# A two-layer transformer block in float32 by split products: in the second layer the high weights take both token parts in one 512-column product

## The chip, the cores and the metric

The kernel runs on one core of one Trainium2 chip. The metric is the time of one execution on the device in microseconds (us); smaller is better. Three runs of the kernel before took 2539.17, 2540.15 and 2541.22 us, a median of 2540.15 us.

## The reference, cut to what matters

Two streams of 256 tokens with 1024 features each, latent and context, go through two layers. Each layer is a half feed-forward block, a mixer and another half feed-forward block. After the mixer of the second layer only the latent stream is used.

```python
DEPTH, D_MODEL, SEQ, CTX_LEN, FF = 2, 1024, 256, 256, 2816

def _swiglu(h, w_in, w_out):
    a, b = jnp.split(h @ w_in, 2, axis=-1)
    return (jax.nn.silu(a) * b) @ w_out

def _half_ffn(h, shift, scale, gate, w1, w2, g, b):
    y = _swiglu(h * (1 + scale) + shift, w1, w2)
    return _layer_norm(DN_ALPHA * h + 0.5 * gate * y, g, b)

def _gated_merge(branches, gates, w_branch, w_out):
    g = jax.nn.sigmoid(gates.reshape(B, T, N_BRANCH, D_MODEL))
    proj = jnp.einsum('btkw,kwd->btkd', br, w_branch)
    return jnp.einsum('btkd,btkd->btd', g, proj) @ w_out

for l in range(DEPTH):
    last = l == DEPTH - 1
    xl = _half_ffn(xl, ...); xc = _half_ffn(xc, ...)
    yl, yc = _mixer(hl, hc, rows, cols, not last, ...)   # LRU, windowed GQA, MLA, retention, merged
    xl = _half_ffn(_layer_norm(DN_ALPHA * xl + ml[5] * yl, ...), ...)
    if not last:
        xc = ...                                         # the same for the context
```

## The kernel before, in words

Activations are kept transposed: a tile has 128 features on the partitions and tokens in the free dimension, latent in columns 0 to 255 and context in 256 to 511. A float32 product is made of three float32r products. Every operand is split into a high and a low part (`split` for activations, `load_w` for weights: ScalarE casts the high part, VectorE subtracts it to get the low part), and `mm3` issues high weights times high tokens (L189), high weights times low tokens (L190) and low weights times high tokens (L191). Such a group of three is called a triple here. The low times low product is dropped.

`gemm_cols` walks a weight matrix in pairs of 128-column blocks. Weights come in units of 512 KB (four feature tiles by 256 columns) over SyncE's DMA queue into three raw buffers and go through the split into four buffers of high and low parts. A pair accumulates in two of four PSUM tiles called `acc`, and then a function of the caller takes each block out of PSUM (the eviction): a ScalarE activation for `silu`, `tanh` and plain copies, a VectorE operation where two operands meet (L568 in the feed-forward block, L1170 in a merge).

In the first layer nearly all products have 512 columns. In the second layer the query-side products of the mixer (`bq`, `cq`, `ay`, `dq`, `dg`, the gates `gt`, the branch projections and `w_out`) and the whole second feed-forward block `ffn11` are for the latent stream alone, so their three products have 256 columns each. There are 1128 such triples: 528 in `ffn11`, 408 against the mixer's input (56 in `gqa_in`, 32 in `lru_out`, 64 in `ret`, 64 in each of the four merges), 128 against the branches (32 in each merge) and 64 in `finish`.

Names that come back below: `gqa_in` makes queries and keys of the windowed attention, `lru` is a VectorE-heavy recurrence that is interleaved with the gate products of `merge1`, `mla` is the second attention, `ret` the retention, `finish` the product with `w_out` and its LayerNorm. A scheduler at build time sets the order of each engine's instructions from the program and its own estimates; on the chip each engine then works its list strictly in that order.

## Time and profile before

| | |
|---|---|
| median of three runs | 2540.15 us (2539.17 to 2541.22) |
| span of the profiled execution | 2538.8 us |
| TensorE busy, modelled | 2453.9 us, 97% |
| TensorE weight loads busy | 2046.2 us, 81% |
| VectorE busy | 1620.2 us, 64% |
| ScalarE busy | 1048.8 us, 41% |
| GpSimd busy | 390.6 us, 15% |
| granted TensorE clock, mean | 0.990 of 2.4 GHz |

No time of the profiled execution is listed other than its span. It lies 1.35 us below the median of the runs, so changes that are worked out against the span are added to the median as they are. PE is TensorE, PEld its weight loads, DVE VectorE, ACT ScalarE, POOL GpSimd and SP SyncE. A line number such as L189 is a line of the kernel before. The busy time of TensorE counts the length of each matmul, and neighbours overlap, so it says that matmuls were in flight and not how fast they follow one another.

### The profile page before, as it was taken

The numbers are of one execution on the slowest core, as the hardware profiler recorded it, in microseconds if no ns is written. First come the engines' busy times: TensorE is split into PE (matmuls) and PEld (weight loads), VectorE is DVE, ScalarE is ACT, GpSimd is POOL, SyncE is SP. The second block draws the span as 40 slices with busy tenths as digits, with TensorE's granted clock in tenths as the row PEclk, the third lists the DMA queues.
The fourth block names the chain that finished last, engine by engine and source line by source line (L and its number), as shares of the span: only waits on it lengthen the run. The fifth ranks groups of instructions, "written<-read, shape, count | busy, mean of one in ns | idle before, by whom it ended". The sixth has DMA issues, their size and how long they took to land.

```text
span 2538.8 us, 35128 instructions
## 1 busy us (share of the span) xinstructions
PE 2453.9 (97%) x13320; PEld 2046.2 (81%) x13320; DVE 1620.2 (64%) x3288; ACT 1048.8 (41%) x1694; POOL 390.6 (15%) x411
## 2 busy tenths in 40 slices
PE   8999999999999999999999999999999999999997
PEld 5888788666776778898877898877886777998997
DVE  4756438768757676467665386664387986766554
ACT  4322226556435322352223252223265754455443
POOL 2000024003111112350000230000240121223002
PEclk9999999999999999999999999999999999999999
DMA  7554334122423334426554346664352342465653
GB/s 262 167 157 149 125 106 149 36 75 84 126 85 91 93 107 138 136 84 190 155 166 141 96 139 210 196 193 156 100 149 68 92 126 75 119 186 162 190 179 113
DMA packets 304027, 340.75 MB, mean 134 GB/s; under 512 B 13505, under 2 KB 262625, under 8 KB 303857
## 3 DMA queue, kind: packets, MB, share of 16 engines
q1 hardware_dynamic: 299600, 323.88, 42.0%
q0 software_dynamic: 4256, 14.63, 1.6%
q8 instruction: 104, 1.70, 0.3%
q14 instruction: 67, 0.54, 0.1%
HBM read 334.26 MB, written 4.20 MB: 133 GB/s over the span
## 4 chain that ended last, share of the span: by engine, by line
PE 69%; DVE 12%; DMA 12%; issue 3%; ACT 3%; POOL 1%; SPq 0%; POOLq 0%; DVEq 0%; ACTq 0%
DMA ffn10.mraw<-in_w_modT 4%; PE ffn01.acc L189 3%; PE ffn01.acc L191 3%; PE ffn01.acc L190 3%; DMA ffn00.mraw<-in_w_modT 3%; PE ffn00.acc L189 3%; PE ffn00.acc L191 3%; PE ffn00.acc L190 3%; PE ffn11.acc L189 3%; PE ffn11.acc L190 3%; PE ffn11.acc L191 3%; DMA ffn01.mraw<-in_w_modT 2%; PE ffn10.acc L189 2%; PE ffn10.acc L190 2%; PE ffn10.acc L191 2%
## 5 line engine op out<-in xcount | busy, mean ns | idle before, releaser
L189 PE MATMUL ffn10.acc<-xh,ffn10.hi 128*128 128x512 f32 (+1 forms) x384 | 141.9, 376 | 7.2 <-DVE ffn10.sa L568 5.0
L189 PE MATMUL ffn01.acc<-xh,ffn01.hi 128*128 128x512 f32 (+1 forms) x384 | 140.5, 374 | 7.9 <-DVE ffn01.sa L568 7.9
L176 ACT CAST ffn10.hi<-ffn10.raw 128x1024 fp32r<-128x1024 f32 (+1 forms) x71 | 72.7, 1024 | 173.4 <-DMA ffn10.raw<-in_ffn_w_in 95.8
L190 PE MATMUL ffn10.acc<-xl,ffn10.hi 128*128 128x512 f32 (+1 forms) x384 | 142.2, 373 | 0.0
L191 PE MATMUL ffn10.acc<-xh,ffn10.lo 128*128 128x512 f32 (+1 forms) x384 | 142.1, 373 | 0.0
L190 PE MATMUL ffn01.acc<-xl,ffn01.hi 128*128 128x512 f32 (+1 forms) x384 | 141.3, 372 | 0.0
L191 PE MATMUL ffn01.acc<-xh,ffn01.lo 128*128 128x512 f32 (+1 forms) x384 | 141.1, 372 | 0.0
L189 PE MATMUL ffn00.acc<-xh,ffn00.hi 128*128 128x512 f32 x336 | 133.4, 398 | 4.7 <-ACT ffn00.hi L176 2.8
L177 DVE TENSOR_TENSOR ffn10.lo<-ffn10.raw,ffn10.hi 128x1024 fp32r<-128x1024 f32 (+1 forms) x71 | 87.4, 1231 | 74.6 <-ACT ffn10.hi L176 74.5
L176 ACT CAST ffn01.hi<-ffn01.raw 128x1024 fp32r<-128x1024 f32 (+1 forms) x71 | 72.6, 1023 | 148.5 <-DMA ffn01.raw<-in_ffn_w_in 70.9
L177 DVE TENSOR_TENSOR ffn01.lo<-ffn01.raw,ffn01.hi 128x1024 fp32r<-128x1024 f32 (+1 forms) x71 | 87.9, 1239 | 72.0 <-ACT ffn01.hi L176 70.3
L177 DVE TENSOR_TENSOR ffn00.lo<-ffn00.raw,ffn00.hi 128x1024 fp32r<-128x1024 f32 (+1 forms) x71 | 86.4, 1218 | 73.0 <-ACT ffn00.hi L176 72.8
L190 PE MATMUL ffn00.acc<-xl,ffn00.hi 128*128 128x512 f32 x336 | 132.3, 394 | 0.0
L191 PE MATMUL ffn00.acc<-xh,ffn00.lo 128*128 128x512 f32 x336 | 132.0, 394 | 0.0
L177 DVE TENSOR_TENSOR ffn11.lo<-ffn11.raw,ffn11.hi 128x1024 fp32r<-128x1024 f32 x68 | 82.3, 1211 | 75.7 <-ACT ffn11.hi L176 75.7
L176 ACT CAST ffn00.hi<-ffn00.raw 128x1024 fp32r<-128x1024 f32 (+1 forms) x71 | 72.4, 1023 | 136.5 <-PE ffn00.acc L190 88.5
L401 DVE SCALAR_TENSOR_TENSOR ffn10.ht<-ffn10.mraw,ffn10.sb 128x512 bf16<-128x512 f32 x128 | 83.6, 687 | 66.3 <-DMA ffn10.mraw<-in_w_modT 62.6
L401 DVE SCALAR_TENSOR_TENSOR ffn01.ht<-ffn01.mraw,ffn01.sb 128x512 bf16<-128x512 f32 x128 | 82.3, 688 | 67.8 <-DMA ffn01.mraw<-in_w_modT 67.7
L401 DVE SCALAR_TENSOR_TENSOR ffn00.ht<-ffn00.mraw,ffn00.sb 128x512 bf16<-128x512 f32 x96 | 62.1, 687 | 70.3 <-DMA ffn00.mraw<-in_w_modT 70.3
L189 PE MATMUL ffn11.acc<-xh,ffn11.hi 128*128 128x256 f32 x352 | 99.7, 287 | 4.8 <-ACT xh L246 4.8
L190 PE MATMUL ffn11.acc<-xl,ffn11.hi 128*128 128x256 f32 x352 | 100.3, 286 | 0.0
L191 PE MATMUL ffn11.acc<-xh,ffn11.lo 128*128 128x256 f32 x352 | 100.1, 286 | 0.0
(682 smaller groups left out, 7826.1 us busy)
## 6 DMA issues: line engine op xcount, KB each, us to landing
ffn10.mraw<-in_w_modT SPq DMA_DIRECT2D x48, 512.0 KB, 4.2
ffn00.raw<-in_ffn_w_in SPq DMA_DIRECT2D x44, 512.0 KB, 3.7
ffn01.raw<-in_ffn_w_in SPq DMA_DIRECT2D x44, 512.0 KB, 4.5
ffn10.raw<-in_ffn_w_in SPq DMA_DIRECT2D x44, 512.0 KB, 4.6
...
```

The costliest lines, as they stand in the source:

```text
L176: nc.scalar.copy(out=hi[:, :n], in_=raw[:, :n])
L177: nc.vector.tensor_tensor(out=lo[:, :n], in0=raw[:, :n], in1=hi[:, :n].bitcast(F32), op=ALU.subtract)
L189: mm(out, wh, xh, start=start, stop=False)
L190: mm(out, wh, xl, start=False, stop=False)
L191: mm(out, wl, xh, start=False, stop=stop)
L401: nc.vector.scalar_tensor_tensor(out=junk, in0=raw[:, e], scalar=1.0, in1=sb[:, i], op0=ALU.mult, op1=ALU.mult, accum_out=dst)
```

## The change

The high and the low part of a set of tokens no longer lie in two tiles. One tile holds `[stream, part, 256]`, so that for one stream high and low are 512 neighbouring columns. Where a product is for the latent stream alone, the high weights meet these 512 columns in one matmul (PSUM columns 0 to 255 get high times high, 256 to 511 high times low), and the low weights meet the high tokens in a second matmul of 256 columns that adds to the first half. Each such block is then summed over its two halves by a new VectorE reduce, `done`, into a buffer in SBUF, and the caller's eviction reads that buffer. Where a product is for both streams the three matmuls stay, but their 512 columns of tokens are now two runs of 256 that lie 512 columns apart. The pools keep their sizes, save that eight tiles of `g` replace sixteen of `q` in `finish` of the second layer.

```diff
+class Split:
+    def __init__(self, t=None, h=None, l=None):
+        self.t = t
+        if t is None:
+            self.H, self.L = (x.rearrange("p (s t) -> p s t", t=L) for x in (h, l))
+        else:
+            self.H, self.L = t[:, :, 0], t[:, :, 1]
+    def hl(self, s):
+        return None if self.t is None else self.t[:, s]
+def by_stream(x):
+    return x.rearrange("p (s t) -> p s t", t=L)
...
-        def block(a, i, m, units, t):
+        def block(a, i, m, units, s=None):
             sl = slice(i * 128, i * 128 + m)
+            mm = self.nc.tensor.matmul
+            a3 = by_stream(a)
             for kk, h, lw in units:
-                self.mm3(a[:m, t], h[:, sl], lw[:, sl], xh[kk][:, t], xl[kk][:, t], kk == 0, kk == kt - 1)
+                st, sp = kk == 0, kk == kt - 1
+                if s is None:
+                    self.mm3(a3[:m], h[:, sl], lw[:, sl], x[kk].H, x[kk].L, st, sp)
+                elif both:
+                    self.mm3(a3[:m, s], h[:, sl], lw[:, sl], x[kk].H[:, s], x[kk].L[:, s], st, sp)
+                else:
+                    mm(a3[:m], h[:, sl], x[kk].hl(s), start=st, stop=False)
+                    mm(a3[:m, 0], lw[:, sl], x[kk].H[:, s], start=False, stop=sp)
+        def done(a):
+            if both:
+                return a
+            r = self.ht(1)
+            self.nc.vector.tensor_reduce(out=r, in_=a.rearrange("p (x t) -> p t x", x=2), axis=AX.X, op=ALU.add)
+            return r
...
-                evac(b0 + i, a, (0, 1) if both else (0,))
+                evac(b0 + i, done(a), (0, 1) if both else (0,))
...
-        self.xh = [self.p_x.tile([128, T], F32R, name=f"xh{d}") for d in range(KD)]
-        self.xl = [self.p_x.tile([128, T], F32R, name=f"xl{d}") for d in range(KD)]
+        self.x = [Split(self.p_x.tile([128, 2, 2, L], F32R, name=f"x{d}")) for d in range(KD)]
...
-                            t = ph.tile([128, 2, T], F32R, tag=f"{nm}{jp}", bufs=1, name=self.name(nm))
-                            lst.extend([t[:, 0], t[:, 1]])
+                    hid.append(Split(ph.tile([128, len(streams), 2, L], F32R, tag=f"h{j}", bufs=1, name=self.name("h"))))
...
-        mh = [self.q(F32R) for _ in range(KD)]
-        ml = [self.q(F32R) for _ in range(KD)]
+            m = Split(h=self.g(F32R), l=self.g(F32R)) if self.both else Split(
+                self.g(F32R).rearrange("p (s x t) -> p s x t", s=1, x=2))
...
-        bh = [self.p_g.tile([128, n], F32R, tag="br", bufs=8, name=self.name("bh")) for _ in range(4)]
-        bl = [self.p_g.tile([128, n], F32R, tag="br", bufs=8, name=self.name("bl")) for _ in range(4)]
+            b = Split(self.p_g.tile([128, n // L, 2, L], F32R, tag="br", bufs=4, name=self.name("b")))
```

The scheduler also orders VectorE's list anew in the second layer's mixer. The first place is the start of that mixer, where VectorE still normalises the context (rows with `ffn10.ht` and `xl`/`x`) while the first queries come out of PSUM (`gqa_in`). This is VectorE before: the shuffles of the first two query blocks stand among the normalisation.

```order
L519 TENSOR_TENSOR ffn10.ht_15356<-ffn10.ht_15356,ffn10.ht_15350 128x256
L776 STREAM_SHUFFLE gqa_in.ht_15508<-gqa_in.tmp_15506 128x256
L518 TENSOR_TENSOR ffn10.ht_15364<-R,ffn10.pss_15340 128x256
L778 TENSOR_TENSOR gqa_in.ht_15508<-gqa_in.ht_15508,ffn10.cc_15424 128x256
L519 TENSOR_TENSOR ffn10.ht_15364<-ffn10.ht_15364,ffn10.ht_15350 128x256
L247 TENSOR_TENSOR xl_85<-ffn10.ht_15360,xh_77 128x256
L518 TENSOR_TENSOR ffn10.ht_15372<-R,ffn10.pss_15340 128x256
L776 STREAM_SHUFFLE gqa_in.ht_15522<-gqa_in.tmp_15520 128x256
```

And this is VectorE in the changed kernel, at the first reduces of `gqa_in`.

```order
L551 TENSOR_TENSOR ffn10.ht_15388<-R,ffn10.pss_15316 128x256
L552 TENSOR_TENSOR ffn10.ht_15388<-ffn10.ht_15388,ffn10.ht_15326 128x256
L282 TENSOR_TENSOR x_83<-ffn10.ht_15384,x_83 128x256
L237 TENSOR_REDUCE gqa_in.ht_15466<-gqa_in.acc_15420 128x256
L282 TENSOR_TENSOR x_84<-ffn10.ht_15392,x_84 128x256
L809 STREAM_SHUFFLE gqa_in.ht_15470<-gqa_in.tmp_15468 128x256
L237 TENSOR_REDUCE gqa_in.ht_15482<-gqa_in.acc_15421 128x256
L811 TENSOR_TENSOR gqa_in.ht_15470<-gqa_in.ht_15470,ffn10.cc_15400 128x256
L812 TENSOR_TENSOR gqa_in.tmp_15468<-gqa_in.ht_15470,gqa_in.ht_15471 128x256
L809 STREAM_SHUFFLE gqa_in.ht_15486<-gqa_in.tmp_15484 128x256
L237 TENSOR_REDUCE gqa_in.ht_15544<-gqa_in.acc_15498 128x256
```

What moved: the first query block now leaves PSUM, through the reduce, behind the normalisation of all but the last context tile (`x_84` is that one).

The second place is the end of the stretch in which `lru` and `merge1` are interleaved, before `mla`. VectorE before: the last two evictions of `merge1` (L1167) and the low parts of `mla`'s weights stand among the operations of `lru` (L743 to L752).

```order
L1167 SCALAR_TENSOR_TENSOR R<-merge1.sa_17039,merge1.acc_17043 128x256
L752 SCALAR_TENSOR_TENSOR R<-lru.g_16598,R,lru.lu_16640 128x256
L743 SCALAR_TENSOR_TENSOR lru.lu_16650<-lru.lu_16650,lru_in.g_16486 128x512
L1167 SCALAR_TENSOR_TENSOR R<-merge1.sa_17041,merge1.acc_17044 128x256
L744 TENSOR_TENSOR lru.lu_16650<-lru.lu_16650,lru.g_16608 128x512
L177 TENSOR_TENSOR mla.lo_17080<-mla.raw_17077,mla.hi_17079 128x1024
L745 TENSOR_TENSOR lru.lu_16650<-lru.lu_16650,R 128x512
L177 TENSOR_TENSOR mla.lo_17149<-mla.raw_17146,mla.hi_17148 128x768
L750 SCALAR_TENSOR_TENSOR R<-lru.g_16608,lru.lu_16650 128x256
L1002 COPY mla.g_17091<-mla_in.g_16248 64x512
L752 SCALAR_TENSOR_TENSOR R<-lru.g_16608,R,lru.lu_16650 128x256
```

VectorE in the changed kernel, from the last operation of `lru` (L785) on.

```order
L785 SCALAR_TENSOR_TENSOR R<-lru.g_16542,R,lru.lu_16584 128x256
L196 TENSOR_TENSOR merge1.lo_16864<-merge1.raw_16861,merge1.hi_16863 128x1024
L196 TENSOR_TENSOR merge1.lo_16886<-merge1.raw_16883,merge1.hi_16885 128x1024
L196 TENSOR_TENSOR merge1.lo_16918<-merge1.raw_16915,merge1.hi_16917 128x1024
L1034 COPY mla.g_16956<-mla_in.g_16182 32x512
L237 TENSOR_REDUCE merge1.ht_16905<-merge1.acc_16859 128x256
L196 TENSOR_TENSOR mla.lo_16946<-mla.raw_16943,mla.hi_16945 128x1024
L237 TENSOR_REDUCE merge1.ht_16909<-merge1.acc_16860 128x256
L196 TENSOR_TENSOR mla.lo_17015<-mla.raw_17012,mla.hi_17014 128x768
L237 TENSOR_REDUCE merge1.ht_16937<-merge1.acc_16913 128x256
L237 TENSOR_REDUCE merge1.ht_16940<-merge1.acc_16914 128x256
```

What moved: the low parts of the last three weight units of `merge1` and the last four of its sixteen reduces now stand behind the last operation of `lru`, and so do both of `mla`'s first low parts.

## Rows read from the trace of the kernel before

**Rows 1.** The page: span, and busy time, share and instructions of each engine.
```profile
span 2538.8 us, 35128 instructions
PE 2453.9 (97%) x13320; PEld 2046.2 (81%) x13320; DVE 1620.2 (64%) x3288; ACT 1048.8 (41%) x1694; POOL 390.6 (15%) x411
```
**Rows 2.** Matmul groups by shape: line, engine, operands, count, busy us, mean ns.
```profile
L189 PE MATMUL ffn00.acc<-xh,ffn00.hi 128*128 128x512 f32 x336 | 133.4, 398 | 4.7 <-ACT ffn00.hi L176 2.8 <-DVE ffn00.sa L568 1.9
...
L190 PE MATMUL ffn11.acc<-xl,ffn11.hi 128*128 128x256 f32 x352 | 100.3, 286 | 0.0
```
**Rows 3.** Timeline of TensorE in `ffn11`: start us, length us, instruction.
```profile
2400.01 0.28 PE L189 MATMUL ffn11.acc<-xh,ffn11.hi 128*128 128x256 f32 x1
2400.14 0.28 PE L190 MATMUL ffn11.acc<-xl,ffn11.hi 128*128 128x256 f32 x1
2400.26 0.28 PE L191 MATMUL ffn11.acc<-xh,ffn11.lo 128*128 128x256 f32 x1
```
**Rows 4.** Stretches: length; busy us (instructions) PE, PEld, DVE, ACT, POOL; clock, DMA.
```profile
150.00:200.00 50.00, 50.00 (x223) 41.39 (x222) 29.54 (x66) 12.53 (x17) 0.00 (x0) 1.00 0.49 151
200.00:250.00 50.00, 50.00 (x222) 41.42 (x221) 28.89 (x64) 15.12 (x19) 0.00 (x0) 1.00 0.50 157
...
2400.00:2450.00 50.00, 50.00 (x419) 50.00 (x418) 28.18 (x38) 23.73 (x36) 0.00 (x0) 1.00 0.59 185
```
**Rows 5.** Stretches of the second layer, same columns: gqa_in, lru/merge1, mla, ..., finish, ffn11.
```profile
1867.40:1907.80 40.40, 34.95 (x221) 30.85 (x220) 35.31 (x79) 27.50 (x56) 17.59 (x20) 0.96 0.51 153
1965.00:2050.50 85.50, 77.48 (x453) 63.39 (x453) 83.67 (x133) 56.63 (x77) 13.20 (x13) 0.96 0.30 87
2050.50:2079.00 28.50, 27.89 (x177) 20.40 (x177) 20.01 (x50) 19.04 (x40) 3.18 (x5) 1.00 0.36 100
2079.00:2088.00 9.00, 9.00 (x66) 8.46 (x65) 6.54 (x11) 6.31 (x10) 4.04 (x7) 1.00 0.69 227
2088.00:2183.00 95.00, 94.04 (x599) 78.85 (x599) 65.51 (x140) 40.57 (x70) 19.29 (x15) 1.00 0.34 94
2183.00:2228.80 45.80, 45.38 (x335) 42.55 (x334) 34.21 (x60) 22.00 (x35) 10.68 (x10) 1.00 0.50 141
2228.80:2263.30 34.50, 34.50 (x290) 34.50 (x289) 20.37 (x25) 16.65 (x24) 6.91 (x9) 1.00 0.65 184
2263.30:2321.00 57.70, 57.70 (x482) 57.60 (x480) 36.65 (x48) 30.40 (x46) 24.18 (x29) 1.00 0.65 201
2328.90:2458.20 129.30, 129.30 (x1055) 129.24 (x1056) 74.47 (x104) 66.33 (x100) 4.62 (x7) 0.98 0.56 172
2458.20:2521.70 63.50, 63.50 (x531) 63.45 (x529) 28.49 (x31) 24.37 (x30) 12.88 (x11) 1.00 0.46 142
```
**Rows 6.** VectorE groups by shape near a reduce of 512 columns.
```profile
L792 DVE TENSOR_REDUCE gqa.st<-gqa.pss 128x1 f32<-128x512 f32 x32 | 21.8, 687 | 0.3
...
L792 DVE TENSOR_REDUCE gqa.st<-gqa.pss 128x1 f32<-128x256 f32 x16 | 6.8, 422 | 7.7 <-PE gqa.pss L836 7.4
...
L745 DVE TENSOR_TENSOR lru.lu<-lru.lu,R 128x512 f32<-128x512 f32 x8 | 8.4, 1055 | 0.1
...
L292 DVE TENSOR_REDUCE sel<-ident 128x2 f32<-128x8 f32 x1 | 0.2, 166 | 4.1 <-DMA ident<-in_cc 4.1
```
**Rows 7.** Timeline of VectorE in `lru`: start us, length us, instruction.
```profile
2018.25 0.68 DVE L731 SCALAR_TENSOR_TENSOR lru.lu<-R,lru.g 128x512 f32<-128x512 f32 x1
2018.85 0.41 DVE L730 TENSOR_SCALAR lru.g<-lru.lu 128x512 f32<-128x512 f32 x1
...
2043.95 0.73 DVE L752 TENSOR_TENSOR_SCAN R<-lru.g,R,lru.lu 128x256 f32<-128x256 f32 x1
```
**Rows 8.** Timeline in `gqa_in`: VectorE's last context tile, TensorE's wait; bracket: idle before.
```profile
1890.52 0.42 DVE L519 TENSOR_TENSOR ffn10.ht<-ffn10.ht,ffn10.ht 128x256 f32<-128x256 f32 x1
...
1900.83 0.57 PE L189 MATMUL gqa_in.acc<-xh,gqa_in.hi 128*128 128x512 f32 x1 [4.83 <-ACT gqa_in.q L939]
```
**Rows 9.** VectorE's low parts in the same stretch: count, ns min/median/max, first and last start.
```profile
L177 DVE TENSOR_TENSOR merge1.lo<-merge1.raw,merge1.hi x12: 1210/1217/1723, 1964.6 to 2027.0; 128x1024 fp32r<-128x1024 f32 x12
```

More of the change, by code (lines that the diff above doesn't have):

```diff
@@ L240, in gemm_cols @@
                     a = self.acc()
-                    block(a, 0, 128, units, halves[s][1])
+                    block(a, 0, 128, units, s)
                     evac(b, a, (s,))
@@ L585, in ev_y @@
                 self.ln_after(ss, after)
[L587 removed]
+            self.gemm_cols(w2, KF, 0, D, hid, tok, ev_y, last=True)
     def prologue(self, ph, w1):
         nc = self.nc
[L593 removed]
+        scr = ph.tile([128, 2, T], F32, tag="h8", bufs=1, name=self.name("scr"))
         ct = scr[:, 0, 128:144].rearrange("p (k i) -> p k i", i=2)
@@ L598, in prologue @@
         nc.scalar.activation(out=self.s32[:, :, 0:2], in_=ct, func=AF.Silu)
-        tags = [f"{nm}{jp}" for jp in range(5, KF // 2) for nm in ("hh", "hl")]
+        tags = [f"h{j}" for j in range(10, KF)]
         cols = [0, FF, 256]
@@ L672, in ev @@
             self.ln_after(ss, after)
-        self.gemm_cols(self.ins["w_out"][l], KD, 0, D, mh, ml, tq, ev, last=True)
+        self.gemm_cols(self.ins["w_out"][l], KD, 0, D, ms, tq, ev, last=True)
     def proj(self, name, ncols, tok, evac, off=0, first=False):
-        self.gemm_cols(self.win, KD, OFF[name] + off, ncols, self.xh, self.xl, tok, evac, first=first)
+        self.gemm_cols(self.win, KD, OFF[name] + off, ncols, self.x, tok, evac, first=first)
     def lru_in(self):
```

52 lines of the change are left out of this document (26 added, 26 removed).

## The prediction

> **What bounds the kernel now.** I read the page first: TensorE is busy 2453.9 of 2538.8 us, VectorE 1620.2 [rows 1]. So the change, which takes a matmul out of each latent-only triple and gives VectorE a reduce per block, must be read as a trade between those two engines, stage by stage. Second, the matmul groups, to see what a matmul costs: 286 ns with 256 columns, 398 with 512 [rows 2]. The reader is to see that these are not prices: in the timeline of `ffn11` a matmul that lasts 0.28 us is followed by the next one after 0.13 and 0.12 us [rows 3]. The price is the pace, from stretches in which TensorE is full at a granted clock of 1.00 (2.4 GHz): 419 matmuls of 256 columns in 50 us are 119.3 ns each, and 223 and 222 of 512 columns are 224.7 ns each [rows 4]. Third, the stretches of the second layer [rows 5]: in `merge2`, `merge3` with `finish`, and `ffn11` TensorE is busy all the time; in the stretch of `lru` and `merge1` VectorE is the bound, with 83.67 of 85.50 us, and TensorE has holes; in `gqa_in` neither engine is full (34.95 and 35.31 of 40.40) and they wait for each other.
>
> **What the change saves.** A triple costs 3 x 119.3 = 357.9 ns. The new pair costs 224.7 + 119.3 = 344.0. That is 14 ns a triple, not the 286 x 3 - 398 - 286 = 174 ns that the means suggest: the three products have as many columns as before, and only what a matmul costs beyond its columns goes away once. All 1128 triples at 14 ns are 15.8 us. It counts where TensorE sets the pace: `ffn11` 528 x 14 = 7.4; `merge2` and `merge3` 192 x 14 = 2.7; `finish` 64 x 14 = 0.9; the products of `ret`, in a stretch where TensorE is busy 94.04 of 95.00 us, 64 x 14 = 0.9. Sum 11.9 us. In `gqa_in`, `merge1`, `lru_out` and `merge0` I count nothing, since there VectorE or a wait is about as late as TensorE.
>
> The Trainium skill has another size for this term ("TensorE: Matmul & The Clock Gate", section "Back-to-back issue gap"): by its formula a matmul takes its columns at 2.4 GHz plus 2.5 ns, so that one fewer per triple would save 2.5 ns x 1128 = 2.8 us. The trace disagrees: 256 columns are 106.7 ns at 2.4 GHz and pace at 119.3, 512 are 213.3 and pace at 224.7, so 11 to 13 ns come with each matmul. By the page's rule the sum below would come out 9 us later.
>
> **What a reduce costs.** There are 143 new reduces, each reading 512 columns of PSUM and writing 256. None of this form is in the trace. The nearest row is a reduce of 512 columns out of PSUM, 687 ns long [rows 6]. VectorE's operations overlap too: one that lasts 0.68 us is followed after 0.60 [rows 7], so I take 0.60 us of VectorE's time. Below, 422 ns, the reduce of 256 columns (0.34 occupied); above, 1055 ns, the slowest operation on 512 columns [rows 6] (0.97 occupied). The one strided reduce of the trace has 8 elements and takes 166 ns, which says little on the stride. The evictions that now read SBUF instead of PSUM I leave at their price (bounds: 0.1 us less or more each; they lie beside other work wherever TensorE is full).
>
> Where TensorE is full, VectorE has room for them. In the long stretch of `ffn11` it has 74.5 us of work, 44 reduces add 26.4, making 101 against TensorE's 129.3 - 5 = 124. `merge2`: 20.4 + 16 x 0.6 = 30.0 of 33.2. `merge3` with `finish`: 36.7 + 24 x 0.6 = 51.1 of 55.5. In the stretch with most of `merge0`, 34.2 + 9.6 = 43.8 of 45.8, is cover that nearly fails; I charge 1.5 us there (0 to 5). At 0.97 a reduce the two merge stretches and `merge0` would be out of cover, which is rival D.
>
> **What a reduce costs on the path.** Each eviction now waits for a reduce on VectorE's list, and with it whatever stands behind.
>
> `gqa_in`: in the order after, the first query block is reduced only behind the normalisation of all but the last context tile. Before, that tile's normalisation ran at 1890.52, and TensorE had a stall of 4.83 us of its own later, at 1900.83 [rows 8]. The two blocks that hold their PSUM until then keep the next pair waiting. Seven reduces at 0.6 are 4.2 us, and part of the old stall takes them up: +2.5 us (from -1, where the other stall shrinks as much, to +7).
>
> `lru` and `merge1`, the largest term. VectorE has 1.8 us of room in 85.5 [rows 5] and gets 16 x 0.6 = 9.6 us. By the order after, 12 of the 16 reduces come ahead of the last operation of `lru` (7.2 us), and about as much moves behind it: three low parts of `merge1` at 1.2 us [rows 9], `mla`'s two, two evictions and a copy. So `lru` ends when it did: the scan at 2043.95 takes 0.73 us [rows 7], giving 2044.7, with 0.2 for the balance 2044.9. But now the last three low parts of `merge1`, on which 24 triples of TensorE wait, begin there. The first is ready 1.2 us later, 24 triples at 0.344 take 8.3, to 2054.4, and only then comes the product of `mla` that was already done at 2050.5 before. A second such product fills 9.0 us [rows 5], so 2063.4 instead of 2050.5: +12.9 us. It is 9.6 (all of VectorE's added work, late but no later) if the order costs nothing more, and 3 if TensorE takes the product of `mla` ahead of the last blocks of `merge1` for some other reason; above, 17, if `mla`'s low parts behind the reduces come late as well. None of this can be regained by TensorE: what follows until 2183 is a chain of attention steps in which it has under 2 us of holes.
>
> `lru_out`: 4 reduces in 28.5 us with VectorE at 20.0, TensorE nearly full: part shows, +1.5. `ret`: 8 reduces, one at the end of each pair: +0.5. Ends of chains with nothing to hide behind: `finish`, a reduce ahead of the LayerNorm, +0.6; the last block of `ffn11`, where two reduces stand ahead of the last two residuals, +1.0.
>
> Sum of costs: 2.5 + 12.9 + 1.5 + 0.5 + 1.5 + 0.6 + 1.0 = 20.5 us. Net 20.5 - 11.9 = +8.6: span 2547.4 instead of 2538.8, and with the 1.35 us between span and median, about 2549 us.
>
> **Rivals.** A difference under 0.2%, 5.1 us, is what a measurement of this kernel can't tell from none: below 2535.1 is faster, above 2545.2 slower.
>
> B, the costs about cancel. The stretch of `lru` loses only 5 us, since VectorE's other work there gets shorter waits (the evictions no longer touch PSUM), and `gqa_in` nothing: 5 + 5.1 for the rest - 11.9, or about 2539 to 2543. For it speaks that the 12.9 us rest on one place of the order, so that a shorter reduce (0.34 us) or a low part that comes a little earlier takes several us off; against it, that 9.6 us are added to an engine with 1.8 us of room.
>
> C, faster. All reduces lie beside TensorE's work, and the holes that TensorE has in the `lru` stretch (85.50 - 77.48 = 8.0 us) take up the late blocks because `lru`'s end, not `merge1`'s, is what `lru_out` and all behind it need. Then only TensorE's gain is left: 2540.2 - 11.9 + 1 = about 2529. It decides if the first product after the `lru` stretch starts within 2 us of where it did. Against it: the order itself puts `mla`'s product behind.
>
> D, slower: the reduce is slow, because its two operands lie 1 KB apart in PSUM. At the upper bound of 0.97 us each of the 31 on VectorE's path (16 of `merge1`, 7 of `gqa_in`, 4 of `lru_out`, 4 at ends) costs 0.37 more, 11.5 us. The three merge stretches come to 34.2 + 20.4 + 36.7 = 91.3 us of VectorE and 56 x 0.97 = 54.3 of reduces, 145.6 against 138 - 3.6 of TensorE, +11. `ffn11` stays covered (74.5 + 42.7 = 117 of 124). Together 2549 + 22 = 2571. From about 0.8 us a reduce the merges turn to VectorE.
>
> [...]
>
> E, slower: in the products for both streams tokens are now two runs of 256 columns. By the program there are 2150 x 3 = 6450 such matmuls; if the break costs a third of what a matmul costs beyond its columns, 4 ns, that is 26 us, or 2575. No row speaks for it or against it.
>
> **Chances.** Forecast 0.50, with its own range 2543 to 2557; B 0.17; C 0.17; D 0.11; E 0.05. Faster: 0.16 from C and 0.02 from B, 0.18. The same: 0.14 from B, 0.05 from the low end of the forecast, 0.01 from C, 0.20. Slower: 0.45 + 0.01 + 0.11 + 0.05 = 0.62. The range leaves out half of C, half of D and E, 0.19: 2532 to 2568.
>
> **What would show it.** In the full stretch of `ffn11` some 290 matmuls in 50 us (100 / 0.344), half of them 512 columns wide, where 419 stood, and the block shorter by 7 us. The new reduce at about 0.69 us long. TensorE's wait for `merge1`'s last low parts after `lru` ends, and `lru_out`'s first matmul 10 to 13 us later against `merge1`'s first. A first-layer pace that stays at 222 to 223 per 50 us. The forecast is wrong if the stretch from `gqa_in` to `mla` is no longer than before, if the reduce is far from 0.6 us, or if the pair in `ffn11` doesn't pace at 344 ns.

## The result: slower by 44 us, and nearly half of it in blocks from which the change takes no product

| | before | after |
|---|---|---|
| median | 2539.98 us (4 runs) | 2584.39 us (4 runs, 2578.14 to 2586.72) |
| ratio | | 1.0165, 95% interval 1.0153 to 1.0177 |
| span of the profiled execution | 2538.8 us | 2576.4 us |

The forecast was 2549 us with a range of 2532 to 2568. The sign was right, the size five times too small. The profiled execution after is the quickest of its four runs (2578.14 us), so the profile accounts for 37.6 us; the other 6.8 of the median I can't place.

The page after, to set beside [rows 1]: 1128 matmuls are gone and 143 VectorE instructions have come.

```profile
span 2576.4 us, 33016 instructions
PE 2454.9 (95%) x12192; PEld 1987.5 (77%) x12192; DVE 1707.8 (66%) x3431; ACT 1053.2 (41%) x1694; POOL 395.0 (15%) x411
```

Busy time does not say where 37.6 us went. I took from both timelines when the first or last product of each block ran, and give how much longer each stretch is in the kernel named than in the kernel before, in us, from one profiled execution of each. (`L1` is everything up to `ffn01`; "lru, mla" reaches to the end of the second product of `mla`, with `lru_out` in it; LN from the last product of `finish` to the first of `ffn11`.) The names in the first column other than "after" are the experiments below.

| | L1 | ffn01 | ffn10 | gqa_in | to lru_in | lru, mla | attention, ret | merge0 | merge2, 3 | finish | LN | ffn11 | sum |
|---|---|---|---|---|---|---|---|---|---|---|---|---|---|
| after | -2.4 | 11.0 | 9.2 | 2.0 | 0.7 | 12.2 | 1.1 | -1.6 | -1.2 | 3.9 | 4.5 | -3.9 | 35.5 |
| layout_only | -0.7 | 0.7 | 2.0 | 0.1 | 0.1 | 0.4 | 0.0 | 0.0 | 0.0 | 0.0 | 0.0 | 0.2 | 2.7 |
| reduce_only | -1.5 | 1.5 | 3.0 | 2.5 | 1.0 | 15.4 | 1.5 | -0.3 | 0.0 | 0.3 | 4.0 | -0.3 | 27.2 |
| no_sum | 0.4 | 12.2 | 9.2 | -1.1 | 0.1 | 0.4 | -0.6 | -0.5 | -2.6 | -0.8 | 0.7 | -6.4 | 10.9 |
| full_stages | -0.7 | 8.4 | 9.4 | 0.1 | 0.0 | 1.6 | 0.0 | 0.0 | -1.3 | 2.5 | 4.4 | -3.7 | 20.6 |
| finish_three | 2.3 | 13.9 | 10.6 | 2.3 | 0.7 | 15.6 | 1.0 | -1.7 | -2.2 | 4.7 | 0.5 | -6.9 | 40.7 |
| after_padded | -8.2 | -2.6 | -1.5 | 3.3 | 0.7 | 11.6 | 1.1 | -1.7 | -1.5 | 4.2 | 4.5 | -4.0 | 6.1 |
| padded | -9.0 | 0.4 | -1.3 | -0.3 | 0.0 | 0.7 | 0.0 | 0.0 | -1.3 | 4.2 | 0.5 | -3.3 | -9.2 |

After the last product come another 2.1 us at the end: 35.5 + 2.1 = 37.6. Three things stand out. `gqa_in` and `lru` with `mla` lost about what was forecast (2.5 and 12.9). `finish` and its LayerNorm lost 8.4 us that were not. And `ffn01` and `ffn10` lost 20.2, where the order of every engine's list is the same as before. `L1` lies between -9.0 and 3.1 in all the kernels of this document, lowest in padded, after_padded and before_tail; no experiment here says why.

**The reduce** has the price that was taken. This is its row in `merge1` (count, ns minimum, median and maximum, first and last start); in the other blocks the median is 679 to 686 ns.

```profile
L237 DVE TENSOR_REDUCE merge1.ht<-merge1.acc x16: 677/682/692, 2010.6 to 2074.6; 128x256 f32<-128x512 f32 x16
```

**`gqa_in`, `lru` and `merge1`.** In `gqa_in` TensorE has a new wait of 7.06 us that ends at a reduce, ahead of its third pair of query blocks, when all four `acc` tiles are taken; the old one of 4.83 us [rows 8], which came later, is gone. And behind the last operation of `lru` TensorE waits for `merge1`'s first low part, with the whole rest of `merge1` and `mla` behind it. TensorE after (start us, length us, instruction, in brackets the idle time before it and what ended it):

```profile
1904.95 0.77 PE L230 MATMUL gqa_in.acc<-x,gqa_in.hi 128*128 128x512 f32 x1 [7.06 <-DVE gqa_in.ht L237]
...
2064.65 0.58 PE L231 MATMUL merge1.acc<-x,merge1.lo 128*128 128x256 f32 x1 [1.90 <-DVE merge1.lo L196]
...
2083.31 0.40 PE L230 MATMUL lru_out.acc<-x,lru_out.hi 128*128 128x512 f32 x1
```

The last of these rows is the first product of `lru_out`. Before it was this one:

```profile
2050.55 0.28 PE L189 MATMUL lru_out.acc<-xh,lru_out.hi 128*128 128x256 f32 x1
```

And VectorE after, at the end of `lru`, against the last row of [rows 7]:

```profile
2062.73 0.74 DVE L785 TENSOR_TENSOR_SCAN R<-lru.g,R,lru.lu 128x256 f32<-128x256 f32 x1
2063.39 4.00 DVE L196 TENSOR_TENSOR merge1.lo<-merge1.raw,merge1.hi 128x1024 fp32r<-128x1024 f32 x3
...
2070.65 0.69 DVE L237 TENSOR_REDUCE merge1.ht<-merge1.acc 128x256 f32<-128x512 f32 x1 [2.81 <-PE merge1.acc L231]
2071.38 1.23 DVE L196 TENSOR_TENSOR mla.lo<-mla.raw,mla.hi 128x1024 fp32r<-128x1024 f32 x1
```

All this lies 20.5 us late from the blocks before (`lru_in` ends that much later). Less that, `lru` ends at 2063.39 - 20.5 = 2042.9 (forecast 2044.9), and `merge1`'s last blocks and `mla` follow it as the order said: `lru_out` starts 32.8 us late, 12.2 of them lost in this stretch. The granted clock in the stretch fell with the longer waits, 0.91 against 0.96 [rows 5], with VectorE nearly as full as before (85.92 of 90.00 us against 83.67 of 85.50):

```profile
1985.00:2075.00 90.00, 72.32 (x301) 52.36 (x301) 85.92 (x140) 53.98 (x72) 12.66 (x13) 0.91 0.24 69
...
2440.00:2490.00 50.00, 50.00 (x285) 43.32 (x284) 39.01 (x55) 24.32 (x36) 0.00 (x0) 1.00 0.61 186
```

The second of these rows (length; busy us and instructions of PE, PEld, DVE, ACT and POOL; clock, DMA) is `ffn11`, where 419 matmuls stood in 50 us [rows 4] and some 290 were expected: 285.

**`finish` and its LayerNorm.** Before, evictions and GpSimd's running sums for the LayerNorm alternated, and the last sum ran at 2321.71 us for 0.73, so that it ended 1.6 us behind the last product. GpSimd before, the last sum and an earlier one:

```profile
2316.66 1.73 POOL L486 TENSOR_TENSOR finish.ss<-finish.ss,R 128x256 f32<-128x256 f32 x1
...
2321.71 0.73 POOL L485 TENSOR_TENSOR finish.ss<-finish.ss,finish.ht 128x256 f32<-128x256 f32 x1
```

After, the residuals come in twos behind two reduces, and the sums in twos behind them. GpSimd after:

```profile
2351.89 2.59 POOL L519 TENSOR_TENSOR finish.ss<-finish.ss,R 128x256 f32<-128x256 f32 x2 [1.07 <-DVE R L494]
2354.44 2.52 POOL L518 TENSOR_TENSOR finish.ss<-finish.ss,finish.ht 128x256 f32<-128x256 f32 x2
2357.32 0.90 POOL L519 TENSOR_TENSOR finish.ss<-finish.ss,R 128x256 f32<-128x256 f32 x1 [0.36 <-DVE R L494]
2358.18 1.70 POOL L518 TENSOR_TENSOR finish.ss<-finish.ss,finish.ht 128x256 f32<-128x256 f32 x1
```

A sum that starts beside one of VectorE's low parts takes up to 1.73 us instead of 0.73, in both kernels: of twelve sums, three took 1.72 or 1.73 before, and five take 1.60 to 1.71 after. What is new is that the sums bunch and that the last of them is a slow one. VectorE is slowed in turn: a low part of 128x1024 that takes 1.22 us alone takes 1.74 here (third row). VectorE, same place:

```profile
2355.49 1.28 DVE L237 TENSOR_REDUCE finish.ht<-finish.acc 128x256 f32<-128x512 f32 x2
2356.69 0.95 DVE L494 SCALAR_TENSOR_TENSOR R<-finish.ht,finish.g,R 128x256 f32<-128x256 f32 x2
2357.56 1.74 DVE L196 TENSOR_TENSOR ffn11.lo<-ffn11.raw,ffn11.hi 128x1024 fp32r<-128x1024 f32 x1
2362.98 0.43 DVE L540 SCALAR_TENSOR_TENSOR finish.ht<-finish.pst,finish.ht 128x256 f32<-128x256 f32 x1 [3.68 <-PE finish.pst L525]
```

So the LayerNorm's statistics wait for the last sum, which ends at 2359.88, 4.2 us behind the last product of `finish` at 2355.7. That is 2.6 of the LayerNorm's 4.5 us. The other 1.9 come behind the last sum. The products for the statistics run at a granted clock of 0.50 after the longer wait, where it was 1.00, and the first product of `ffn11` waits for VectorE's low part of the tokens, where it was ScalarE's high part; I have not split the 1.9 between the two. TensorE before, then after:

```profile
2323.03 0.59 PE L491 MATMUL finish.pss<-R,onesd 128*128 128x256 f32 x2
...
2328.85 1.01 PE L189 MATMUL ffn11.acc<-xh,ffn11.hi 128*128 128x256 f32 x3 [4.79 <-ACT xh L246]
```

```profile
2360.95 1.06 PE L524 MATMUL finish.pss<-R,onesd 128*128 128x256 f32 x2
...
2368.21 0.77 PE L230 MATMUL ffn11.acc<-x,ffn11.hi 128*128 128x512 f32 x1 [5.35 <-DVE x L282]
```

**`ffn01` and `ffn10`.** TensorE's only idle group in `ffn01` is the wait for an eviction (L598), 15.1 us in all against 7.9, which is 7.2 of the 11.0 us that it lost. First after, then before:

```profile
L208 PE MATMUL ffn01.acc<-x,ffn01.hi 128*128 128x512 f32 (+1 forms) x384 | 141.8, 377 | 15.1 <-DVE ffn01.sa L598 15.1
```

```profile
L189 PE MATMUL ffn01.acc<-xh,ffn01.hi 128*128 128x512 f32 (+1 forms) x384 | 140.5, 374 | 7.9 <-DVE ffn01.sa L568 7.9
```

The rest is TensorE itself, which is busy 3.8 us longer with the same products at a granted clock of 0.99 instead of 1.00 (the whole of `ffn01`, after and before, in the columns of [rows 4]):

```profile
1112.80:1499.40 386.60, 371.53 (x1831) 313.96 (x1829) 222.49 (x460) 120.66 (x172) 36.62 (x43) 0.99 0.46 140
```

```profile
1115.20:1490.80 375.60, 367.70 (x1830) 311.63 (x1829) 222.48 (x460) 120.98 (x172) 36.68 (x43) 1.00 0.47 144
```

The eviction is late because it stands on VectorE's list behind products for the modulation, and these wait for their weights, `mraw`. VectorE's group after, and before: the same 128 instructions of 688 ns, but 75.3 us of waiting for the load and not 67.8.

```profile
L435 DVE SCALAR_TENSOR_TENSOR ffn01.ht<-ffn01.mraw,ffn01.sb 128x512 bf16<-128x512 f32 x128 | 82.3, 688 | 75.3 <-DMA ffn01.mraw<-in_w_modT 75.3
```

```profile
L401 DVE SCALAR_TENSOR_TENSOR ffn01.ht<-ffn01.mraw,ffn01.sb 128x512 bf16<-128x512 f32 x128 | 82.3, 688 | 67.8 <-DMA ffn01.mraw<-in_w_modT 67.7
```

The loads themselves take longer from issue to landing (last number, median us; `raw` are the weights of the block): 4.4 against 3.9 in `ffn01`. After, and before:

```profile
ffn10.mraw<-in_w_modT SPq DMA_DIRECT2D x48, 512.0 KB, 4.5
ffn01.raw<-in_ffn_w_in SPq DMA_DIRECT2D x44, 512.0 KB, 4.5
ffn01.mraw<-in_w_modT SPq DMA_DIRECT2D x32, 512.0 KB, 4.4
```

```profile
ffn10.mraw<-in_w_modT SPq DMA_DIRECT2D x48, 512.0 KB, 4.2
ffn01.raw<-in_ffn_w_in SPq DMA_DIRECT2D x44, 512.0 KB, 4.5
ffn01.mraw<-in_w_modT SPq DMA_DIRECT2D x32, 512.0 KB, 3.9
```

In the mean of the 32 loads it is 4.47 us against 4.24. In `ffn10` the median is 4.5 against 4.2, and the mean of 48 loads 4.49 against 4.27. The 44 loads of `raw` shown, of 512 KB too, land after 4.5 us in both kernels. A loop closes here: late load, late eviction, TensorE waits, weight buffers come free late, the next load is issued late. What had made the loads slower is what most experiments went into.

### The profile page after: what moved, and what is told of

Its sections match the earlier page's. It is cut to its first block, busy times and chain, and to the rows that moved or that the text cites. A ratio compares the mean times of both kernels' runs of the same rounds, so it can differ in the third digit from the quotient of the medians.

```text
span 2576.4 us, 33016 instructions
## 1 busy us (share of the span) xinstructions
PE 2454.9 (95%) x12192; PEld 1987.5 (77%) x12192; DVE 1707.8 (66%) x3431; ACT 1053.2 (41%) x1694; POOL 395.0 (15%) x411
## 4 chain that ended last, share of the span: by engine, by line
PE 66%; DVE 14%; DMA 13%; issue 3%; ACT 2%; POOL 1%; SPq 0%; DVEq 0%; POOLq 0%; ACTq 0%
DMA ffn10.mraw<-in_w_modT 5%; PE ffn11.acc L230 5%; DMA ffn01.mraw<-in_w_modT 3%; PE ffn01.acc L208 3%; PE ffn01.acc L209 3%; PE ffn01.acc L210 3%; DMA ffn00.mraw<-in_w_modT 3%; PE ffn00.acc L208 3%; PE ffn00.acc L209 3%; PE ffn00.acc L210 3%; PE ffn11.acc L231 2%; PE ffn10.acc L208 2%; PE ffn10.acc L210 2%; PE ffn10.acc L209 2%; DVE ffn01.ht L435 2%
## 5 line engine op out<-in xcount | busy, mean ns | idle before, releaser
L208 PE MATMUL ffn01.acc<-x,ffn01.hi 128*128 128x512 f32 (+1 forms) x384 | 141.8, 377 | 15.1 <-DVE ffn01.sa L598 15.1
L208 PE MATMUL ffn10.acc<-x,ffn10.hi 128*128 128x512 f32 (+1 forms) x384 | 142.2, 377 | 13.3 <-DVE ffn10.sa L598 11.2
L210 PE MATMUL ffn10.acc<-x,ffn10.lo 128*128 128x512 f32 (+1 forms) x384 | 142.4, 374 | 1.5 <-DVE ffn10.lo L196 1.5
L209 PE MATMUL ffn01.acc<-x,ffn01.hi 128*128 128x512 f32 (+1 forms) x384 | 142.4, 375 | 0.0
L209 PE MATMUL ffn10.acc<-x,ffn10.hi 128*128 128x512 f32 (+1 forms) x384 | 142.2, 373 | 0.0
L210 PE MATMUL ffn01.acc<-x,ffn01.lo 128*128 128x512 f32 (+1 forms) x384 | 142.1, 374 | 0.0
L208 PE MATMUL ffn00.acc<-x,ffn00.hi 128*128 128x512 f32 x336 | 132.4, 395 | 5.6 <-DVE ffn00.sa L598 2.9
L435 DVE SCALAR_TENSOR_TENSOR ffn01.ht<-ffn01.mraw,ffn01.sb 128x512 bf16<-128x512 f32 x128 | 82.3, 688 | 75.3 <-DMA ffn01.mraw<-in_w_modT 75.3
L230 PE MATMUL ffn11.acc<-x,ffn11.hi 128*128 128x512 f32 x352 | 126.2, 404 | 5.3 <-DVE x L282 5.3
L210 PE MATMUL ffn00.acc<-x,ffn00.lo 128*128 128x512 f32 x336 | 131.2, 392 | 0.0
L209 PE MATMUL ffn00.acc<-x,ffn00.hi 128*128 128x512 f32 x336 | 131.1, 391 | 0.0
L195 ACT CAST ffn11.hi<-ffn11.raw 128x1024 fp32r<-128x1024 f32 x68 | 69.6, 1025 | 85.7 <-PE ffn11.acc L230 75.4
L231 PE MATMUL ffn11.acc<-x,ffn11.lo 128*128 128x256 f32 x352 | 98.9, 283 | 0.0
```

The lines of the kernel that those rows point to most:

```text
L195: nc.scalar.copy(out=hi[:, :n], in_=raw[:, :n])
L208: mm(out, wh, xh, start=start, stop=False)
L209: mm(out, wh, xl, start=False, stop=False)
L210: mm(out, wl, xh, start=False, stop=stop)
L230: mm(a3[:m], h[:, sl], x[kk].hl(s), start=st, stop=False)
L231: mm(a3[:m, 0], lw[:, sl], x[kk].H[:, s], start=False, stop=sp)
```

## Experiments

**layout_only, no_sum, reduce_only, full_stages** take the change apart. They are made from the changed kernel, save reduce_only, which is made from the one before.

```diff
 # layout_only, in block() and done()
-mm(a3[:m], h[:, sl], x[kk].hl(s), start=st, stop=False)
-mm(a3[:m, 0], lw[:, sl], x[kk].H[:, s], start=False, stop=sp)
+self.mm3(a3[:m, 0], h[:, sl], lw[:, sl], x[kk].H[:, s], x[kk].L[:, s], st, sp)
-if both:
     return a
```

> The new layout of the token parts stays, but every latent-only triple is three products of 256 columns again, into the first half of PSUM, with no reduce. Theory 1 (the layout by itself, through the two runs of the moving operand or the writes into it, is what makes the first layer's ffn01 and the second layer's ffn10 9 to 11 us longer): about 2540 + 20 = 2560 us, the loads of mraw in ffn01 again land after some 4.4 us (median) and not 3.9. Theory 2 (the loss in ffn01 and ffn10 has nothing to do with the layout, or comes only with the new program's placement of data): 2540 to 2545 us, ffn01 and ffn10 375 and 376 us long as before.

Measured 2541.45 us (2538.93 to 2548.12), ratio 0.9996 (0.9986 to 1.0007). The layout costs nothing that shows, in either layer: rival E, and my first theory, are out.

```diff
 # no_sum, in done()
-if both:
     return a
```

> The changed kernel without the summation: the eviction reads the first half of PSUM directly, so the high times low product is issued but left out of the result. If the reduces and the order that they bring cost about 20 us in the second layer and the pair of products gives back 12, this is 20 us less than the changed kernel's second layer: about 2584 - 21 = 2563 us, with gqa_in to mla no longer than before and ffn11 still some 185 us. If the pair of products gains nothing, and the reduces are hidden, it is as the changed kernel, 2580 to 2584 us. The loss in ffn01 and ffn10 (some 20 us) should be in it by the theory that the layout makes it.

Measured 2554.57 us (2551.84 to 2559.96), ratio 1.0048 (1.0030 to 1.0067). Behind `ffn10` it is 10.9 us quicker than the kernel before (21.8 late at the end of `ffn10`, 10.9 at the end of `ffn11`; forecast for the pairs alone: 11.9). The loss in `ffn01` and `ffn10` is in it, 21.4 us, with no reduce.

```diff
 # reduce_only, on the kernel before (and the new done() as in the change)
+mm(a[:m, 0:L], h[:, sl], xh[kk][:, t], start=st, stop=False)
+mm(a[:m, L:T], h[:, sl], xl[kk][:, t], start=False, stop=False)
+mm(a[:m, 0:L], lw[:, sl], xh[kk][:, t], start=False, stop=sp)
```

> The kernel before with only this: the high times low product goes into PSUM columns 256 to 511, and the 143 reduces sum the halves; three products of 256 columns, old layout. Theory 1 (the layout makes the loss in the first layer): ffn01 and ffn10 as before, the second layer's mixer longer by the price of the reduces and their order, some 20 us: 2555 to 2562 us. Theory 2 (the loss in ffn01 and ffn10 comes with any new program): about 2580 us, with ffn01 and ffn10 longer by 20 us together.

Measured 2568.28 us (2564.44 to 2571.37), ratio 1.0096 (1.0078 to 1.0115): 24 us behind `ffn10`, of it 15.4 in `lru` and `mla`, 4.0 in the LayerNorm, 2.5 in `gqa_in`. Up to the end of `ffn10` it is 3.0 us late.

```diff
 # full_stages
+pair = not both and self.lab in ("ffn11", "finish", "merge2", "merge3")
-elif both:
+elif not pair:
...
-            if both:
+            if not pair:
                 return a
```

> The new layout, with the pair of products and the reduce only where TensorE was full before: ffn11, finish, merge2 and merge3; everywhere else in the second layer three products of 256 columns and no reduce. If the stages add up as in the prediction, the second layer gains 7.4 + 0.9 + 2.7 = 11 us, less 1 or 2 for the reduces at the ends: with the loss in ffn01 and ffn10 (20 us, if the layout makes it) 2540 - 9.5 + 20 = about 2550 us; without that loss about 2530 us.

Measured 2566.55 us (2563.63 to 2568.11), ratio 1.0089 (1.0072 to 1.0106). That is 16 us over the forecast with the loss in it. `gqa_in` is as before and `lru` with `mla` 1.6 us late, but the gain of 5.0 us in `merge2`, `merge3` and `ffn11` is more than eaten by 2.5 us in `finish` and 4.4 in the LayerNorm; and `ffn01` and `ffn10` are slow again. So the slow loads came with the pairs, with or without reduces. What the pairs have in common is that they shorten TensorE's program.

**two_products, low_cut, dram_pad** try that apart from the pairs; **finish_three** tries the LayerNorm.

```diff
 # two_products, on the kernel before, latent-only
-self.mm3(a[:m, t], h[:, sl], lw[:, sl], xh[kk][:, t], xl[kk][:, t], kk == 0, kk == kt - 1)
+mm(a[:m, t], h[:, sl], xh[kk][:, t], start=st, stop=False)
+mm(a[:m, t], lw[:, sl], xh[kk][:, t], start=False, stop=sp)
```

> The kernel before (old layout, no reduce, no 512-column product), but of each of the 1128 latent-only triples the high times low product is left out, so that TensorE's program has as many instructions as the changed kernel's. Theory 1 (it is the shorter program, through where data or code come to lie, and not what the second layer computes, that makes the loads of mraw land later in ffn01 and ffn10): ffn01 and ffn10 are longer by 8 to 11 us each, mraw in ffn01 lands after 4.4 us in the median. Theory 2 (it comes with the 512-column product): 375 and 376 us, mraw after 3.9 us. The second layer is shorter in both by up to 1128 x 0.12 = 135 us, less where weights or VectorE become the bound: about 2420 to 2480 us in all.

Measured 2494.75 us (2490.57 to 2501.00), 15 us over the forecast in the total. `ffn01` and `ffn10` are 9.1 and 11.4 us longer than before, with the old layout and no 512-column product:

```profile
ffn01.mraw<-in_w_modT SPq DMA_DIRECT2D x32, 512.0 KB, 4.4
```

```diff
 # low_cut
-mm(a3[:m, 0], lw[:, sl], x[kk].H[:, s], start=False, stop=sp)
+mm(a[:m, 0:128], lw[:, sl], x[kk].H[:, s, 0:128], start=False, stop=False)
+mm(a[:m, 128:256], lw[:, sl], x[kk].H[:, s, 128:256], start=False, stop=sp)
```

> The changed kernel, but the product of the low weights is cut into two of 128 columns, so that TensorE has as many instructions as before. Theory 1 (the length of the program): ffn01 and ffn10 are back to 375 and 376 us, mraw in ffn01 after 3.9 us, some 18 us saved there; the cut costs 11 to 13 ns x 1128 = up to 14 us in the second layer, less where TensorE waits: 2570 to 2580 us in all. Theory 2 (the 512-column product itself): ffn01 and ffn10 stay 10 us longer each, 2590 to 2600 us in all.

Measured 2672.46 us (2671.19 to 2678.19). The total missed by 90 us, behind `ffn10` (130.3 us late at the end of `ffn11`; below). The question is answered all the same: with the pairs in place and 13320 matmuls, `ffn01` and `ffn10` are 1.0 and 2.6 us from before, and the load is back.

```profile
ffn01.mraw<-in_w_modT SPq DMA_DIRECT2D x32, 512.0 KB, 3.9
```

```diff
 # dram_pad
-self.sd = self.p_d.tile([16, 128], F32, name="sd")
+self.sd = self.p_d.tile([304, 128], F32, name="sd")[0:16]
```

> The changed kernel with one small scratch tensor in DRAM made 147 KB larger, of which nothing more is used; all instructions are the same. If the late loads of mraw come from where data lie in DRAM, this may move them: ffn01 and ffn10 at 375 and 376 us, some 18 us less than the changed kernel, 2565 us. If placement has no part in it, or this tensor does not move w_modT, it is as the changed kernel, 2578 to 2587 us, with mraw in ffn01 after 4.4 us.

Measured 2579.27 us (2577.68 to 2586.41); `ffn01` and `ffn10` 11.6 and 9.0 us longer than before. No effect: this does not show that placement matters, and does not rule it out.

```diff
 # finish_three
+pair = not both and self.lab != "finish"   # and as in full_stages
```

> The changed kernel, but with three products of 256 columns and no reduce in finish alone. Theory 1 (the reduces of finish delay the residuals, GpSimd's sums for the LayerNorm collide with VectorE's low parts and end late): from the end of merge3 to the first product of ffn11 it is some 31 us as before and not 39, so 7 to 8 us less than the changed kernel: about 2576 us. Theory 2 (the LayerNorm is late for another reason, such as the layout of the normalised tokens): the stretch stays 38 to 39 us, 2584 us.

Measured 2575.86 us (2573.72 to 2583.27). The LayerNorm is back to within 0.5 us of before (4.5 in the changed kernel), so the reduces of `finish` are its cause. That the median came out at the 2576 of theory 1 is luck, since the LayerNorm gives back 4.0 us and not 7 to 8; the profiled execution was the slowest of the four, 2583.27 us. `finish` itself stays late, 4.7 us: my theory had put both on the same reduces, and half of it falls. `finish` is 2.5 to 4.7 us late in the kernels above that have pairs and reduces in `merge3`, -0.8 with the pairs alone and 0.3 with the reduces alone; after shows TensorE idle for 2.27 us at its first products, until VectorE has their tokens. Why it takes both I have not settled.

**after_padded, padded, ffn11_pairs, w1_pairs** vary the length of TensorE's program. The padding is tiny matmuls behind the last real one, of which each makes two in the trace:

```diff
 # padding, in ln_add, behind the matmuls for the statistics
+if self.lab == "ffn11":
+    pt = self.acc()
+    for _ in range(1128):      # 720 in padded
+        nc.tensor.matmul(pt[0:32, 0:2], self.onesd[:, 0:32], st["sr"][:, 0:2], start=True, stop=True)
 # pairs, in padded / ffn11_pairs / w1_pairs
+pair = not both and self.lab in ("ffn11", "merge2", "merge3")
+pair = not both and self.lab == "ffn11"
+pair = not both and self.lab == "ffn11" and kt == KD
```

> The changed kernel with 1128 tiny matmuls (32x2 out, result unused) as the last work of TensorE, behind its last matmul for the LayerNorm; everything else is the same. Theory 1 (the length of TensorE's program decides where things lie, and so how late mraw lands): ffn01 and ffn10 375 and 376 us long, mraw in ffn01 after 3.9 us, so that the last block of ffn11 ends 17 to 19 us earlier than in the changed kernel. Theory 2 (the count of instructions ahead of ffn01 and ffn10, or the 512-column product): ffn01 and ffn10 386 us as in the changed kernel. The tiny matmuls themselves run in the last 14 us, in which TensorE was idle, and beyond: at 30 to 120 ns each 34 to 135 us, of which 20 to 120 lengthen the run; the total is read without them.

Measured 2655.90 us; in its trace the tiny matmuls run from 2533.4 to 2653.7. `ffn11` ends 6.1 us later than in the kernel before and not 35.5: the same instructions up to there, 29 us sooner, where 17 to 19 were expected. Of the 29, 24.3 are in `ffn01` and `ffn10` and 5.8 in `L1`.

> Pairs and reduces only in ffn11, merge2 and merge3 (720 triples), three products elsewhere, and 720 tiny matmuls behind TensorE's last one, so that its program is as long as before. If the length of the program is what matters, ffn01 and ffn10 are as before, the second layer gains 720 x 7 to 13 ns = 5 to 9 us less 1 to 2 for the reduces at the end: the last block of ffn11 ends 4 to 7 us earlier than in the kernel before. The tiny matmuls lengthen the end by 8 us (30 ns each) to 70 (120 ns each).

Measured 2596.75 us (2585.33 to 2597.80) with the padding; `ffn11` ends 9.2 us earlier than before. Behind `ffn10` it is 0.7 us slower than before: the 4.6 gained in the merges and `ffn11` are lost again, 4.2 of them in `finish`. The 9.2 come from `L1` (-9.0); `ffn01` and `ffn10` are as before (0.4 and -1.3), as the theory of the length has it.

> Pairs and reduces in ffn11 alone (528 triples), no padding: TensorE has 12792 matmuls, between 12536, where ffn01 and ffn10 were slow, and 13320, where they were not. If the length of the program has one limit between the two, ffn01 and ffn10 are either as before, and then the kernel is 528 x 7 to 13 ns = 4 to 7 us faster less 1 for the end, 2534 to 2538 us; or 8 to 10 us longer each, and then 2550 to 2556 us.

Measured 2555.27 us (2550.66 to 2559.28), ratio 1.0058 (1.0038 to 1.0078): the slow outcome, although `ffn11` gains 6.7 us.

> Pairs and reduces only in the first product of ffn11 (352 triples): 12968 matmuls, no reduce at the end of the program. Same two outcomes: with ffn01 and ffn10 as before 352 x 7 to 13 ns = 2.5 to 4.5 us faster, 2535 to 2538 us; with the late mraw 2552 to 2558 us.

Measured 2547.04 us (2544.62 to 2551.89), ratio 1.0024 (1.0013 to 1.0035): between the two outcomes. So there is no one limit; the loss goes down over a stretch.

**after_pool, before_tail, w1_tail** ask whose length it is and what can be done with it.

```diff
 # after_pool, at the end of run()
+t = self.ht()
+for _ in range(1800):
+    nc.gpsimd.tensor_copy(out=t[:, 0:2], in_=self.R[KD - 1][:, 0:2])
 # before_tail, w1_tail: the padding above with range(160), on the kernel before and on w1_pairs
```

> The changed kernel with 1800 tiny copies on GpSimd behind everything else (they read the last normalised tile, so none runs before the output is there). Theory 1 (the length of the whole program decides how late mraw lands): ffn01 and ffn10 are as before or shorter, 370 to 376 us each, and the last block of ffn11 ends 18 to 29 us earlier than in the changed kernel. Theory 2 (only the length of TensorE's own program counts): ffn01 and ffn10 386 us, as in the changed kernel. The copies lengthen the end by 100 us or more; the total is read without them.

Measured 3027.89 us with the copies. `ffn01` and `ffn10` are 7.9 and 9.8 us longer than before, mraw lands after 4.4 us: 1800 more instructions in GpSimd's program do not bring the loads back, as 2256 more matmuls in TensorE's did.

> The kernel before with 160 tiny matmuls (result unused) behind TensorE's last one, 320 instructions of TensorE's matmul kind at 42 ns each as they ran in the padded kernels, 13 us, in the 14 us at the end in which TensorE was idle. If the length of TensorE's program sets how late mraw lands also above 13320 matmuls, 13640 lie about half way to 14040, where ffn10 ended 9.8 us earlier: 4 to 5 us faster than the kernel before, 2535 to 2537 us. If the length does not matter, or the tail gets longer, 2540 to 2545 us.

Measured 2540.63 us (2534.09 to 2542.51), ratio 1.0000 (0.9991 to 1.0009). No gain: forecast 4 to 5 us, wrong. The 42 ns were wrong too, read from a window that began late: in after_padded and padded a tiny matmul's instruction takes 53 ns. Here the 320 take 14.0 us, with 32 ns each at first and 53 behind the fall of the clock (below).

> Pairs and reduces only in the first product of ffn11 (352 triples), and 160 tiny matmuls (320 in the program) in TensorE's idle end, so that its program has 13288 matmuls, nearly as many as before. If the loss in ffn01 and ffn10 follows the length of TensorE's program, both are 375 to 378 us long again (380 and 381 without the tiny matmuls), and the gain of ffn11 stays, 2 to 4 us: 2536 to 2540 us, just under the kernel before. If the length is not what matters, 2545 to 2550 us as without them.

Measured 2541.89 us (2535.99 to 2550.57), ratio 1.0007 (0.9996 to 1.0018): 5.2 us less than w1_pairs with nothing added but padding in an idle end, and level with the kernel before. The forecast held for `ffn01` (377.2 us) and failed for `ffn10`, 380.6 where w1_pairs had 380.9; and 2.1 us of the difference between the two traces are in `ffn11`, whose pairs ran at one of two paces (below). So this kernel says little by itself of the length. It does not beat the kernel before, and no other version here that computes the whole result does.

In order of the number of matmuls, all kernels together (length of `ffn01` and `ffn10` in us, from first product to first product of the next block, and to the last):

| matmuls in TensorE's program | kernels | ffn01 | ffn10 |
|---|---|---|---|
| 12192 | two_products, no_sum, after, dram_pad, after_pool | 383.5 to 387.8 | 384.8 to 387.2 |
| 12256 to 12792 | finish_three, full_stages, ffn11_pairs | 384.0 to 389.5 | 384.2 to 386.4 |
| 12968 | w1_pairs | 380.4 | 380.9 |
| 13288 | w1_tail | 377.2 | 380.6 |
| 13320 | before, layout_only, reduce_only, low_cut | 375.6 to 377.1 | 375.8 to 378.7 |
| 13640 to 14448 | before_tail, padded, after_padded | 373.0 to 378.0 | 374.3 to 376.9 |

The rows do not overlap across 12792 and 12968, whatever the layout, the order of the second layer or the products are. The median landing of mraw in `ffn01` goes with them: 4.4 to 4.6 us up to 12536 matmuls, 4.2 at 12792, 4.0 and 4.1 at 12968 and 13288, and 3.8 to 3.9 from 13320 on. That the length of TensorE's program decides is shown, by after against after_padded above all. How it does is not: the instructions concerned come long after `ffn10`, so it can't be their execution. Nor is more code loaded meanwhile: on the queue that brings instructions and grows with TensorE's program (96 packets of 16 KB in after, 104 before), `ffn01` and `ffn10` have 14 packets each in every trace. That the length shifts where data or code lie in DRAM, and these loads with it, is a guess.

## Why the prediction was wrong, step by step

- **"The price is the pace."** Right in kind: 1128 fewer matmuls gave 10.9 us (no_sum), not the 200 that the means suggest; forecast 11.9. The pace was read a little too fast, since a window counts the matmuls that are under way at its edges: start to start, 256 columns take 120.0 ns and not 119.3, 512 take 227 and not 224.7. A pair takes 347 ns in no_sum and in dram_pad, but 353 in after, though dram_pad has the same instructions; `ffn11` gained 7.3 us in the one and 3.9 in the other. The forecast of 7.4 is near the one and twice the other. Behind `ffn11` the two reduces cost 2.1 us, not 1.0. `merge2` and `merge3` gained 1.2 where 2.7 was forecast, with pairs at the slower pace; at the quicker one no_sum gained 2.6 and finish_three, with the reduces, 2.2. The formula of the Trainium skill ("TensorE: Matmul & The Clock Gate", section "Back-to-back issue gap") gives 2.8 us for all the pairs; the page states it for an isolated matmul, a condition that the prediction left out. The trace disagrees by a factor of four.
- **"What a reduce costs."** Right: 671 to 693 ns, and no slower for operands 1 KB apart: 687 ns was the row for neighbouring columns [rows 6]. Rival D is out. The Trainium skill ("SBUF — State Buffer", section "Door 1: The DMA port swizzle (why `[64,N]` ≈ `[32,N]`)") says of PSUM's lines of 8 bytes that an access pattern which isn't contiguous slows matmuls down significantly. This VectorE operation shows no such loss.
- **`gqa_in` +2.5, `lru` and `merge1` +12.9.** Right, in mechanism too: +2.0, a new wait of 7.06 us in place of the old 4.83, and +12.2 (11.6 to 16.4 in the kernels with the same reduces). Reading the order was worth more here than any busy share.
- **"`merge0` stage, I charge 1.5 us."** It gained 1.6: cover of 43.8 in 45.8 us held. `lru_out` and `ret`, 2.0 of costs less 0.9 of gain, come to the 1.1 that was measured only by luck: `lru_out` lost nothing, since it and the product behind it are both 12.2 late, and the attention and `ret` lost 1.1 where -0.4 was forecast.
- **"`finish`, a reduce ahead of the LayerNorm, +0.6."** Failed: 8.4 us over `finish` and the LayerNorm, where -0.3 was forecast. I priced one reduce and left out the chain behind it: GpSimd's sums bunch, and collide with VectorE. finish_three and reduce_only show the LayerNorm's 4 us as the price of the reduces in `finish`; the 3.9 us of `finish` itself stay open.
- **The step that failed most is one that is not in the sum.** Stretches from which the change takes no product were given no term, and `ffn01` and `ffn10` were given to rival E, for a reason in TensorE's matmuls; that rival's 2575 us came near by accident, and layout_only refutes it. The loss, 20.2 of 37.6 us, came through loads that wait on nothing of the change: `mraw` lands later when TensorE's program is shorter, and how that comes about stays open. Of the 29.0 us between +8.6 and +37.6 these two blocks are 20.2, and `finish` with the LayerNorm 8.7. In after_padded, with the length gone, the changed kernel's real work ends 6.1 us later than before, close to the +8.6 of the sum; but that is luck, since the figure holds -12.2 up to the end of `ffn10`. Behind it the kernel is 18.3 late, against 7.6 forecast (8.6 less 1.0 for the end). Of the 10.7 between, 9.0 are `finish` and the LayerNorm. None of the three signs that were to show the forecast wrong came: the stretch from `gqa_in` to `mla` is longer, the reduce is 0.68 us long (0.69 expected), the pair paces at 347 to 353 ns. All three looked at places that the change touches.
- **Rival B.** Its sum, 5 + 5.1 - 11.9, gives 2538 us and not 2539 to 2543. Nothing hangs on it.
